# A rotary-embedding kernel on one core: the last load and the first store cut into four DMAs each, and one table copy moved to ScalarE

## The chip, the core and the metric

One core of a Trainium2 chip. The metric is device time in microseconds (us), the median over executions of one program; a profiled execution also gives its span, from the first to the last instruction, which is some 1.7 us shorter than the time. Most executions agree within 0.3%. Now and then one is 1.5 to 2.1 us slower: these are called slow runs and are left out wherever two kernels are compared.

## The reference

```python
x: (8, 8, 1024, 64) float32, freqs: (32,), positions: (1024,), scale = 0.5
angles = np.outer(positions * scale, freqs)             # (1024, 32)
cos, sin = np.cos(angles), np.sin(angles)
x_first, x_second = x[..., :32], x[..., 32:]
out = concatenate([x_first * cos - x_second * sin,
                   x_first * sin + x_second * cos], axis=-1)   # float32
```

16.8 MB are read and 16.8 MB written, and there is little arithmetic for each byte.

## The kernel before

The 64 heads are four units of 16. A unit is a tile of 128 partitions with 8192 elements in each (N = 8192), which is 32 KB of float32 a partition, 4.19 MB in all. The loads that GpSimd issues cast to fp16 on their way: units 1 to 3 and the first half of unit 0. Its second half comes as float32, issued by SyncE and ScalarE. VectorE multiplies and adds in fp16, ScalarE copies the result to a float32 tile OUT, and that is stored: units 0 and 1 from GpSimd, one DMA each, units 2 and 3 from SyncE in halves.

```python
    # ... tiles, and unit 0's second half to X0f by SyncE and ScalarE (cut)
    pin(nc.gpsimd.dma_start(out=Xf[0][:, :NH], in_=xv[0][:, :NH]))
    # ... small constants for the tables (cut)
    for u in range(1, NU):
        pin(nc.gpsimd.dma_start(out=Xf[u], in_=xv[u]))
    # ... angles, sine and cosine on few rows (cut)
    for g in range(0, G, 2):                 # 8 rounds: TensorE spreads the tables over the partitions
        ps = spread.tile([P, 2, 2, W], FP32, tag="g")
        # ... two matmuls (cut)
        if g in (0, 4):
            pin(nc.vector.tensor_copy(out=dst, in_=ps))
        else:
            pin(nc.scalar.copy(out=dst, in_=ps))
    pin(nc.scalar.copy(out=Xf[0][:, NH:], in_=X0f[:, :NH]))

    for u in range(NU):
        OUT = xout.tile([P, N], FP32, tag="O")       # 3 buffers
        for s in range(2):
            # ... four VectorE instructions on half s of X[u] (cut)
            pin(nc.scalar.copy(out=OUT[:, ns], in_=Xf[u][:, ns]))
            if u >= NU // 2:
                pin(nc.sync.dma_start(out=ov[u][:, ns], in_=OUT[:, ns]))
        if u < NU // 2:
            pin(nc.gpsimd.dma_start(out=ov[u], in_=OUT))
```

The whole kernel:

## Time and profile before

| | before |
|---|---|
| time, median | 84.51 us (84.47 to 84.59) |
| span of the profiled execution | 82.8 us |
| VectorE, ScalarE busy | 73%, 49% |
| DMA queues' packets, share of 16 engines' time | 66.4 + 27.2 + 3.2 = 96.8% |
| landings of units 1, 2, 3 and of unit 0's store | 22.62, 32.32, 42.98, 52.74 us |

How to read it: two engines look half free, but the DMA engines are never free. The lines that carry this are in the prediction below. The number to keep is the distance between two landings, called a *step* here: 4.19 MB take 9.70 us when the stream runs well, and the step from unit 2 to unit 3, the last load, was 10.66 us.

One warning on the windows: a packet counts where it starts, with the bytes it writes. A load that casts thus shows 216 GB/s when it reads 432, and one microsecond can show a DMA share above 1 when many long packets start in it.

### The profile page before, as it was taken

Reading aid. Unit: us, or ns where it says so; the run is one execution under the profiler, and the core shown is the slowest. Engines: PE = TensorE matmul, PEld = TensorE weight load, DVE = VectorE, ACT = ScalarE, POOL = GpSimd, SP = SyncE. Lnnn points to the kernel's source line nnn. Section 1 sums busy time; section 2 is a strip of 40 time slices with the busy share of each in tenths; the row PEclk is TensorE's granted clock in tenths of the full one; section 3 lists DMA queues with packets and bytes.
Section 4 is the critical chain, followed back from the end, with each engine's and each line's share of the span. In section 5 each row is a group of like instructions: output and inputs, shape, how many; then the busy total and the mean of one; then the engine's idle time right before and its main releaser. Section 6 shows DMA issues by size and latency. Waiting matters only on the chain.

```text
span 82.8 us, 179 instructions
## 1 busy us (share of the span) xinstructions
PE 7.0 (8%) x18; PEld 2.7 (3%) x18; DVE 60.3 (73%) x40; ACT 40.1 (49%) x18; POOL 4.6 (6%) x14
## 2 busy tenths in 40 slices
PE   0011799200000000000000000000000000000000
PEld 0011233000000000000000000000000000000000
DVE  0306276999999999999999999999999997000000
ACT  0602159999960690294088049209606912950000
POOL 4920000000000002000000200000000000000000
PEclk9999999975555555555555555555555555555555
DMA  2899998997999899699979989999899999999991
GB/s 40 335 326 269 293 333 182 253 238 150 246 253 198 182 253 238 143 253 253 127 301 459 507 348 412 507 443 420 380 436 420 412 420 436 444 420 436 428 428 55
DMA packets 1874, 26.22 MB, mean 317 GB/s; under 512 B 338, under 2 KB 338, under 8 KB 338
## 3 DMA queue, kind: packets, MB, share of 16 engines
q0 software_dynamic: 864, 15.73, 66.4%
q1 hardware_dynamic: 720, 9.44, 27.2%
q10 hardware_dynamic: 290, 1.06, 3.2%
HBM read 16.79 MB, written 16.78 MB: 406 GB/s over the span
## 4 chain that ended last, share of the span: by engine, by line
DVE 55%; ACT 14%; issue 6%; DMA 6%; PE 5%; DVEq 1%; ACTq 0%
DVE pr L152 19%; DVE X L153 19%; DVE X L157 9%; DVE X L154 6%; DMA freq_row<-in_freqs_dram 6%; ACT T L139 5%; ACT OUT L160 4%; PE ps L129 4%; ACT X L140 4%; DVEq L195 1%; PE cfreq L97 1%; ACT tab L122 1%; DVE r L113 1%; DVE y L104 1%; ACTq L69 0%
## 5 line engine op out<-in xcount | busy, mean ns | idle before, releaser
L160 ACT CAST OUT<-X 128x4096 f32<-128x4096 f16 x8 | 28.8, 3606 | 24.2 <-DVE X L157 24.2
L152 DVE TENSOR_TENSOR pr<-X,T 128x4096 f16<-128x4096 f16 x8 | 18.3, 2292 | 1.0 <-ACT T L139 0.7
L153 DVE TENSOR_TENSOR X<-X,T 128x4096 f16<-128x4096 f16 x8 | 18.3, 2292 | 0.3
L154 DVE TENSOR_TENSOR X<-X,pr 128x2048 f16<-128x2048 f16 x8 | 9.8, 1225 | 0.3
L157 DVE TENSOR_TENSOR X<-pr,X 128x2048 f16<-128x2048 f16 x8 | 9.7, 1219 | 0.0
L139 ACT CAST T<-ps 128x1024 f16<-128x1024 f32 x6 | 5.7, 1030 | 2.6 <-PE ps L129 2.6
L129 PE MATMUL ps<-tab,sel 128*128 128x512 f16 x16 | 6.4, 584 | 2.2 <-ACT tab L122 2.2
L137 DVE CAST T<-ps 128x1024 f16<-128x1024 f32 x2 | 2.5, 1225 | 2.2 <-PE ps L129 2.2
L140 ACT CAST X<-X0f 128x4096 f16<-128x4096 f32 x1 | 3.7, 3651 | 0.0
L164 POOL DMA_DIRECT2D out_dram<-OUT x2 | 1.1, 536 | 40.3 <-ACT OUT L160 40.3
L95 DVE COPY sel<-one 128x2048 f16<-128x2048 f16 x1 | 0.7, 693 | 2.8 <-POOL one L87 2.8
L117 ACT ACTIVATE tab<-r 128x256 f16<-128x256 f32 x1 | 0.4, 416 | 4.3 <-DVE r L113 4.3
L129 PEld LDWEIGHTS <-sel 128*128 128x128 f16 x16 | 2.2, 138 | 6.0 <-issue 5.8
L117 ACT ACT_TABLE_LOAD x1 | 1.3, 1283 | 2.1 <-issue 2.1
L92 POOL DMA_DIRECT2D X<-in_x_dram x3 | 2.0, 658 | 0.0
L100 DVE CAST posf<-pos_i 128x8 f32<-128x8 int32 x1 | 0.2, 172 | 2.3 <-DMA pos_i<-in_positions_dram 2.3
L97 PE MATMUL cfreq<-freq_row,coef 1*128 1x32 f32 x2 | 0.6, 392 | 5.9 <-DMA freq_row<-in_freqs_dram 5.9
L104 DVE TENSOR_TENSOR y<-posf,cfreq 128x256 f32<-128x256 f32 x1 | 0.4, 422 | 0.5 <-PE cfreq L97 0.5
L83 POOL DMA_DIRECT2D X<-in_x_dram x1 | 0.7, 667 | 0.8 <-POOLq L181 0.8
L97 PEld LDWEIGHTS cfreq<-freq_row,coef 1*128 1x128 f32 x2 | 0.5, 305 | 5.8 <-issue 5.8
L122 ACT ACTIVATE tab<-ra,quarter 128x256 f16<-128x256 f32 x1 | 0.5, 507 | 0.0
L113 DVE SCALAR_TENSOR_TENSOR r<-m,y 128x256 f32<-128x256 f32 x1 | 0.4, 424 | 0.0
(10 smaller groups left out, 1.9 us busy)
## 6 DMA issues: line engine op xcount, KB each, us to landing
out_dram<-OUT POOLq DMA_DIRECT2D x2, 4096.0 KB, 20.8
out_dram<-OUT SPq DMA_DIRECT2D x4, 2048.0 KB, 11.6
X<-in_x_dram POOLq DMA_DIRECT2D x3, 2048.0 KB, 28.7
X0f<-in_x_dram SPq DMA_DIRECT2D x1, 1024.0 KB, 4.8
X<-in_x_dram POOLq DMA_DIRECT2D x1, 1024.0 KB, 11.7
X0f<-in_x_dram ACTq DMA_DIRECT2D x1, 1024.0 KB, 12.2
pos_i<-in_positions_dram ACTq DMA_DIRECT2D x1, 8.0 KB, 5.0
freq_row<-in_freqs_dram ACTq DMA_DIRECT2D x1, 0.1 KB
```

The source lines that it names most:

```text
L92: pin(nc.gpsimd.dma_start(out=Xf[u], in_=xv[u]))
L97: nc.tensor.matmul(out=cfreq, lhsT=coef, rhs=freq_row, start=True, stop=True)
L117: pin(nc.scalar.activation(out=tab[:, 0], in_=r, func=AF.Sin, bias=0.0, scale=-_TWO_PI_DN))
L129: nc.tensor.matmul(out=ps[:, i].rearrange("p t w -> p (t w)"), lhsT=sel[:, g + i].rearrange("s h q -> s (h q)"), rhs=tab.rearrange("s t k ...
L137: pin(nc.vector.tensor_copy(out=dst, in_=ps))
L139: pin(nc.scalar.copy(out=dst, in_=ps))
L140: pin(nc.scalar.copy(out=Xf[0][:, NH:], in_=X0f[:, :NH]))
L152: pin(nc.vector.tensor_tensor(out=pr, in0=Xs, in1=sin_b, op=ALU.mult))
L153: pin(nc.vector.tensor_tensor(out=Xs, in0=Xs, in1=cos_b, op=ALU.mult))
L154: pin(nc.vector.tensor_tensor(out=Xs[:, :, 0, :], in0=Xs[:, :, 0, :], in1=pr[:, :, 1, :], op=ALU.subtract))
L157: pin(nc.vector.tensor_tensor(out=Xs[:, :, 1, :], in0=pr[:, :, 0, :], in1=Xs[:, :, 1, :], op=ALU.add))
L160: pin(nc.scalar.copy(out=OUT[:, ns], in_=Xf[u][:, ns]))
```

## The change

The kernel is bound by its DMA stream, and the stream loses about one microsecond where loads turn to stores. The intent, as far as the diff tells it, was to shrink what is in flight there: unit 3 is loaded and unit 0 is stored in four DMAs each, with rows of 8 KB instead of 32 KB (counted in float32). Beside it one of VectorE's two table copies goes to ScalarE.

```diff
     for u in range(1, NU):
-        pin(nc.gpsimd.dma_start(out=Xf[u], in_=xv[u]))
+        parts = 4 if u == NU - 1 else 1
+        for i in range(parts):
+            c = slice(i * N // parts, (i + 1) * N // parts)
+            pin(nc.gpsimd.dma_start(out=Xf[u][:, c], in_=xv[u][:, c]))
...
-        if g in (0, 4):
+        if g == 0:
             pin(nc.vector.tensor_copy(out=dst, in_=ps))
...
         if u < NU // 2:
-            pin(nc.gpsimd.dma_start(out=ov[u], in_=OUT))
+            parts = 4 if u == 0 else 1
+            for i in range(parts):
+                c = slice(i * N // parts, (i + 1) * N // parts)
+                pin(nc.gpsimd.dma_start(out=ov[u][:, c], in_=OUT[:, c]))
```

## The prediction

> **What bounds the kernel now.** I read the page first (busy shares, the 40 slices, the DMA queues), then the chain of work that ended last, then the landings of single DMAs, then windows of one to ten microseconds, and at the end the packet records. The page:
>
> ```profile
> DVE  0306276999999999999999999999999997000000
> DMA  2899998997999899699979989999899999999991
> q0 software_dynamic: 864, 15.73, 66.4%
> q1 hardware_dynamic: 720, 9.44, 27.2%
> q10 hardware_dynamic: 290, 1.06, 3.2%
> HBM read 16.79 MB, written 16.78 MB: 406 GB/s over the span
> ```
>
> The VectorE line stops at four fifths of the span while the DMA line never stops, and the shares of the three queues add up to 96.8% of the 16 DMA engines' time. The rest, 3.2% of 82.8 us or 2.6 us, is the start (the first packet begins at 1.75 us) and the end (the last one ends at 81.5 us). So the DMA engines carry packets without a gap. 33.57 MB in 79.75 us is 421 GB/s.
>
> The chain of work names VectorE for 55% of the span, but it ends with the last ScalarE copy, which starts at 69.84 us and takes 3.60 us, and 9 us of stores are still to come. The issues by window show who waits at the end (stores of unit 3, first and second half; the columns are KB and us to landing):
>
> ```profile
> out_dram<-OUT SPq DMA_DIRECT2D x1, 2048.0 KB, 10.5
> ...
> out_dram<-OUT SPq DMA_DIRECT2D x1, 2048.0 KB, 8.4
> ```
>
> The first was issued at 66.47 us and lands at 77.0, the second at 73.47 and lands at 81.9. A half takes 4.86 us of the engines, so the second was moved straight after the first and had waited for it. Issue to first packet took 1.0 us where the queue was empty (0.74 to 1.75 us at the start), so VectorE and ScalarE could end some 2.5 us later and change nothing. The bound is the DMA stream alone, and a gain counts only if that stream gets shorter.
>
> Is the stream at one rate? The windows (columns PE, PEld, DVE, ACT, POOL, clock, DMA share, GB/s; a packet counts where it starts, and a load that casts to fp16 counts at its written half):
>
> ```profile
> 22.70:32.40 9.70, 0.00 (x0) 0.00 (x0) 9.53 (x7) 4.92 (x2) 0.54 (x1) 0.50 1.01 216
> 32.40:42.10 9.70, 0.00 (x0) 0.00 (x0) 9.56 (x7) 4.05 (x2) 0.00 (x0) 0.50 1.00 196
> ...
> 43.00:52.70 9.70, 0.00 (x0) 0.00 (x0) 9.56 (x6) 5.87 (x2) 0.53 (x1) 0.50 1.00 432
> ```
>
> Unit 2's load moves 216 GB/s of fp16, which is 432 of source; unit 0's store moves 432. Unit 3's load, the last one, manages 196 although its engines are just as busy. Single landings say the same: unit 1 at 22.62 us, unit 2 at 32.32, unit 3 at 42.98, unit 0's store at 52.74. The steps are 9.70, 10.66 and 9.76 us. So there is one blemish of 0.96 us, and it lies exactly where the loads end and the stores begin:
>
> ```profile
> 40.00:41.00 1.00, 0.00 (x0) 0.00 (x0) 1.00 (x2) 0.00 (x0) 0.00 (x0) 0.50 2.01 262
> 41.00:42.00 1.00, 0.00 (x0) 0.00 (x0) 0.97 (x2) 0.34 (x1) 0.00 (x0) 0.50 0.00 0
> 42.00:43.00 1.00, 0.00 (x0) 0.00 (x0) 1.00 (x1) 1.00 (x1) 0.00 (x0) 0.50 1.25 524
> ```
>
> All 16 engines start the last row of the load between 40.2 and 40.7 us and none starts another packet before 42.04. The packet records have the last row of each engine at 2.01 us on average and the one before at 1.41, where every other row took 1.227: 0.78 + 0.18 = 0.96 us, the step again. I see no other loss in the stream.
>
> **What the Trainium skill says.** "DMA: Bandwidth & Descriptors", section "Where 436 GB/s comes from", gives 435.2 GB/s as what the fabric lets 16 DMA engines move. The 432 GB/s above agree: in the steady parts nothing is left, so only the changeover can be gained. The same page, "Anatomy of one DMA", gives each DMA about 2.0 us of fixed cost, mostly the wait for the receipt. Six more DMAs would then be 12 us if exposed; but on one queue the trace shows landings 9.70 us apart for 4.19 MB, which is 432 GB/s with the completion inside, so it is hidden. "Why small descriptors are slow", also there, speaks of about 3 cycles a packet and 32 bytes a descriptor; against 8 KB that is little, and the trace agrees: 16 KB rows of one store follow each other every 0.607 us on an engine, 32 KB rows every 1.209. "SBUF — State Buffer", in its box on DVE blocking DMA, warns that GpSimd can't write descriptors while VectorE holds the shared port. Not seen here: both GpSimd stores were issued in 0.53 to 0.54 us while VectorE was 96% busy.
>
> **The change part by part.**
>
> *Six more DMAs on GpSimd.* Each costs GpSimd about 0.54 us. The three more loads end near 6.3 us instead of 4.7; the engines reach unit 3 at 32.3 us. The stores: the listing of the changed kernel's order has the second to fourth quarter wait for semaphores that units 0 to 2's loads used before. These land at 13, 22.6 and 32.3 us, so the last quarter is issued by about 33.9 us at the latest, and the engines reach it after 42. Worth 0.
>
> *More packets.* Unit 3's load and unit 0's store go from 128 rows each to 512, and there are 6 x 16 = 96 more semaphore packets: 768 + 96 = 864 more, so q0 should show 1,728. Rows: 16 KB against 32 KB costs 2 x 0.607 - 1.209 = 0.005 us a 32 KB row. With two and three times that for 8 KB, 0.010 to 0.015 us, over 8 rows an engine and two units: 0.16 to 0.24 us. Semaphores: an engine's next row comes 0.022 us later where one DMA ends on the load queue, 0.006 to 0.009 in the stores: 3 x 0.022 + 3 x 0.008 = 0.09 us. Sum: +0.25 to +0.33 us, all on the path, as the engines have no gap.
>
> *The changeover.* A store that SyncE issued at 52.33 us got its first packet at 55.82, when GpSimd's store had 32 KB rows in flight; 1.0 us is its issue, so an engine seems to have one to two rows committed ahead. My reading: near the end of the load an engine already fetches the store's first row from SBUF beside the load's last row from HBM, so the last load row gets only part of the read side, and the write side starves; 0.96 us is 0.79 of a 32 KB row's 1.209 us. If what is committed ahead is counted in rows, 8 KB rows lose a quarter: 0.24 us, a gain of 0.72. If it is counted in bytes, the gain is 0. I hold the first for likelier, some 60 to 40. This is the step on which the sign depends.
>
> *The table copy.* VectorE's copies take 1.23 us each, at 9.75 and 11.46; ScalarE's 1.03:
>
> ```profile
> L139 ACT CAST T<-ps 128x1024 f16<-128x1024 f32 x6 | 5.7, 1030 | 2.6 <-PE ps L129 2.6
> L137 DVE CAST T<-ps 128x1024 f16<-128x1024 f32 x2 | 2.5, 1225 | 2.2 <-PE ps L129 2.2
> ```
>
> ScalarE's first ends at 11.6 and it then waits until 12.31, so the moved copy fills that hole. With ScalarE's own spacing of 0.93 to 0.94 us (three in 2.80 us) the copy now at 12.31 starts near 12.48: the first product on VectorE, ScalarE's copy of X0f and everything after them come 0.17 us later. VectorE gets 1.23 us freer in a stretch where it waits for that copy anyway. Against 2.5 us of slack at the end: 0.
>
> *Sum.* Counted in rows: -0.72 + 0.29 = -0.4 us. Counted in bytes: +0.3 us.
>
> **The rivals.**
> (a) The changeover loss stays, as it is one of bytes in flight or of HBM turning from reads to writes: 84.8 us. For it speaks that all engines slow down together around 40 us; against it, that the slowdown begins before any store packet.
> (b) Rows of 8 KB at a pitch of 32 KB in memory run slower: unit 3 and unit 0 at 10% less would be +2 us, 86.5. Against it: X0f was loaded in just such rows and took 0.313 us each on a busy engine, a 64-byte packet of the other queue between two of them included, which is no loss.
> (c) VectorE or a buffer takes over as the bound: unit 3's output goes into unit 0's buffer, but unit 0's store lands at 52.7 and the buffer is wanted at 62.8. VectorE needs unit 3 at 55.7 and it lands near 42.6. Slack of 10 us or more, so I give this little.
> (d) The loss disappears wholly and rows cost nothing: 83.5 us.
>
> **Range and chances.** 84.51 - 0.4 in the likelier case, + 0.3 in the other: I say 84.2 us. The range is 83.6 (nearly all of the 0.96 us back) to 85.0 (nothing back and rows half as dear again as estimated). A verdict of faster needs 82.8, so 1.7 us, more than the one blemish holds; slower needs 86.2, which only (b) or something unseen gives. Chances: faster 0.03, same 0.93, slower 0.04.
>
> **What would show it.** The step from unit 2's landing to unit 3's last landing falls from 10.66 to about 10.0 us if rows count, and stays near 10.7 or more if bytes do; no whole microsecond near 41 us without a packet start; q0 with 1,728 packets; the stores of unit 0 within 9.76 + 0.2 us of the last load; the first product on VectorE near 13.5 us; the last store issued near 73.6 us, still behind another. I'd be wrong if small rows run below 432 GB/s, if the quarters wait on GpSimd, or if the end comes to hang on VectorE.

## The result, and the profile after

The time went from 84.51 us to 84.69 us (84.58 to 84.96), six fast runs each. The ratio is 1.0022, with a 95% interval of 1.0006 to 1.0037: the change costs about 0.2 us, within 2%. Ratios here and below are the mean time of one kernel's fast runs over that of the other's fast runs of the same rounds, so they are not quite the ratio of the medians quoted.

The page of the changed kernel; the lines are those that the prediction shows of before (queues: packets, MB, share of 16 engines):

```profile
DVE  0306416999999999999999999999999995000000
DMA  2899997997999798999999999989999899999991
...
q0 software_dynamic: 1728, 15.73, 67.1%
q1 hardware_dynamic: 720, 9.44, 27.1%
q10 hardware_dynamic: 290, 1.06, 3.2%
```

The 1,728 packets are there, and the same 15.73 MB took 67.1% of a span of 82.9 us where they had taken 66.4% of 82.8. The shares add up to 97.4%: still no gap. The same microseconds as before (columns PE, PEld, DVE, ACT, POOL, clock, DMA share, GB/s):

```profile
40.00:41.00 1.00, 0.00 (x0) 0.00 (x0) 1.00 (x2) 0.00 (x0) 0.00 (x0) 0.50 1.05 127
41.00:42.00 1.00, 0.00 (x0) 0.00 (x0) 0.97 (x2) 0.51 (x1) 0.00 (x0) 0.50 1.03 131
42.00:43.00 1.00, 0.00 (x0) 0.00 (x0) 1.00 (x1) 1.00 (x1) 0.00 (x0) 0.50 0.99 352
```

Before, the slow row was one packet, so that its slowness showed only as a hole. With short rows the same stretch is resolved four times as finely, and it is not a hole but a slope: for two microseconds the load ran at 127 to 131 GB/s of fp16, instead of the 217 that it showed from 36 to 38 us, with every engine busy. The loss was made visible, not made smaller. The landings of unit 3's four quarters, issued at 4.13, 4.65, 5.17 and 5.69 us (columns KB, us to landing):

```profile
X<-in_x_dram POOLq DMA_DIRECT2D x1, 512.0 KB, 30.6
X<-in_x_dram POOLq DMA_DIRECT2D x1, 512.0 KB, 32.6
X<-in_x_dram POOLq DMA_DIRECT2D x1, 512.0 KB, 34.6
X<-in_x_dram POOLq DMA_DIRECT2D x1, 512.0 KB, 37.4
```

That is 34.77, 37.23, 39.73 and 43.06 us in the trace's record of semaphores. The quarters follow each other by 2.46, 2.46 and 2.50 us, and the last one by 3.33. The step from unit 2 to the end of unit 3 is 10.75 us (before: 10.66), the step of unit 0's store 9.87 (before: 9.76). The two differences, 0.09 and 0.11 us, add up to the 0.2 us of the result; they come from one profile each, and the run of the table copy below shows that the second repeats well and the first does not.

### The profile page after: what moved, and what is told of

The parts are those of the page before. It is cut to its first block, busy times and chain, and to the rows that moved or that the text cites. A ratio compares the mean times of both kernels' runs of the same rounds, so it can differ in the third digit from the quotient of the medians.

```text
span 82.9 us, 192 instructions
## 1 busy us (share of the span) xinstructions
PE 6.9 (8%) x18; PEld 2.7 (3%) x18; DVE 59.1 (71%) x39; ACT 41.0 (49%) x19; POOL 7.8 (9%) x20
## 3 DMA queue, kind: packets, MB, share of 16 engines
q0 software_dynamic: 1728, 15.73, 67.1%
q10 hardware_dynamic: 290, 1.06, 3.2%
## 4 chain that ended last, share of the span: by engine, by line
DVE 54%; ACT 17%; issue 7%; DMA 5%; PE 3%; DVEq 1%; ACTq 0%
DVE X L156 19%; DVE pr L155 19%; DVE X L160 9%; ACT T L142 7%; DMA freq_row<-in_freqs_dram 5%; DVE X L157 5%; ACT OUT L163 4%; ACT X L143 4%; PE ps L132 2%; DVEq L201 1%; PE cfreq L100 1%; ACT tab L125 1%; DVE r L116 1%; DVE y L107 1%; ACTq L69 0%
## 5 line engine op out<-in xcount | busy, mean ns | idle before, releaser
L142 ACT CAST T<-ps 128x1024 f16<-128x1024 f32 x7 | 6.5, 1043 | 2.0 <-PE ps L132 2.0
L170 POOL DMA_DIRECT2D out_dram<-OUT x5 | 2.7, 537 | 37.0 <-ACT OUT L163 36.3
L95 POOL DMA_DIRECT2D X<-in_x_dram x6 | 3.5, 612 | 0.0
L140 DVE CAST T<-ps 128x1024 f16<-128x1024 f32 x1 | 1.2, 1225 | 1.7 <-PE ps L132 1.7
L83 POOL DMA_DIRECT2D X<-in_x_dram x1 | 0.7, 669 | 0.8 <-POOLq L187 0.8
```

The lines of the kernel that those rows point to most:

```text
L95: pin(nc.gpsimd.dma_start(out=Xf[u][:, c], in_=xv[u][:, c]))
L170: pin(nc.gpsimd.dma_start(out=ov[u][:, c], in_=OUT[:, c]))
```

## The experiments

Eleven kernels ran, one of them twice. All gave correct results. The times of before that stand beside each run are those taken on the same chip. Three theories were to be told apart:

- **P, read-ahead.** The engines read a part of the coming store beside the last rows of the load. The load slows down for as long as that takes. It happens when a store stands behind the load, and once.
- **R, rows.** As P, but what is read ahead is counted in rows, so short rows shrink it. This was the likelier case of the prediction.
- **T, turning.** Memory or engine pays each time that the direction turns from reads to writes. **E**, a cousin: the last rows of any queue of loads are slow by themselves. **W**, which comes in with the later runs: any store that waits behind a load slows its last rows, however small it is.

### One part of the change at a time

Only the loads:

```diff
+        parts = 4 if u == NU - 1 else 1      # loop as in the change; store and table copy as before
```

> Only unit 3's load is split into four DMAs of 8 KB rows. If the loss where loads end and stores begin counts bytes (theory P: the engines read a fixed amount of the coming store beside the last of the load), it stays: step from unit 2's landing to unit 3's last landing 10.7 to 10.8 us, and the kernel 0.05 to 0.15 us slower than before (24 rows more an engine at 0.003 us and 3 semaphores at 0.022 us are 0.14 us). If it counts rows of the load (theory R): step near 10.1 us and 0.4 us or more faster.

Measured: 84.59 us against 84.55, ratio 1.0004 (0.9987 to 1.002). Step to unit 3: 10.59 us, of which 0.14 are the shorter rows and the semaphores; so the loss is 10.59 - 9.69 - 0.14 = 0.76 us (9.69 is the step without any loss, measured below). R's 10.1 us and 0.4 us gained did not come.

Only the store:

```diff
+            parts = 4 if u == 0 else 1       # loop as in the change; loads and table copy as before
```

> Only unit 0's store is split into four DMAs of 8 KB rows. Theory P: the step to unit 3's landing stays 10.66 us, the store's own step grows from 9.76 to about 9.87 us, the kernel is about 0.1 us slower. Theory R, counting rows of the store: step near 10.0 us and 0.5 us faster. If e1 and e2 together make up the 0.2 us of the whole change, nothing is left for the table copy.

Measured: 84.77 us against 84.55, ratio 1.0027 (1.0014 to 1.0041). Of the three parts this is the only one whose interval leaves out no change at all. That of the loads alone reaches 1.002, so some of the cost can lie there too.

Only the table copy:

```diff
-        if g in (0, 4):
+        if g == 0:
```

> Only the table copy goes to ScalarE. Every theory: the last store is issued with some 2.5 us to spare, so the time is that of before within 0.05 us; the first product on VectorE starts 0.1 to 0.2 us later than before, counted from the start of the sine. More than 0.1 us of change would say that the end does hang on VectorE.

Measured: 84.61 us against 84.55, ratio 1.0008 (0.9996 to 1.0021), no difference that the runs can tell. VectorE's first product started 5.74 us after the sine (13.54 and 7.80 us) where it had been 5.61 (13.36 and 7.75), so 0.13 us later, and nothing came of it. VectorE and ScalarE have time to spare at the end, as the prediction read from the landings. This run also tells how well a step repeats, as its loads and stores are those of before. The store's step is the same, 9.75 us. The step to unit 3 is 10.60 us where the profile of before has 10.66; by the middle one of the 16 engines instead of the last it is 10.50 where before has 10.69. A difference of 0.1 to 0.2 us between two single profiles of this step therefore tells nothing.

### Four turns instead of one

The eight DMAs of the change, in another order on GpSimd: load quarter, store quarter, four times; q4(i) stands for the i-th quarter of the columns.

```diff
+    pin(nc.gpsimd.dma_start(out=Xf[3][:, q4(0)], in_=xv[3][:, q4(0)]))        # after units 1 and 2
...
+            for i in range(4):                                                # after unit 0's products
+                pin(nc.gpsimd.dma_start(out=ov[0][:, q4(i)], in_=OUT[:, q4(i)]))
+                if i < 3:
+                    pin(nc.gpsimd.dma_start(out=Xf[3][:, q4(i + 1)], in_=xv[3][:, q4(i + 1)]))
```

> The same eight DMAs as in the changed kernel, but in the order load quarter, store quarter, four times, so that loads turn to stores four times instead of once. Theory P: what is read ahead is read ahead once and stays ahead, so the loss comes once and the time is that of the changed kernel, 84.5 to 84.9 us. Rival T (memory or engine pays 0.9 us at each turn from reads to writes): three more turns, 84.7 + 2.7 = 87.4 us.

Measured: 84.85 us against 84.55, ratio 1.0034 (1.0022 to 1.0046). T wanted 87.4 us; it falls. Windows of this kernel, within the four quarters of unit 3's load (last column GB/s, fp16):

```profile
32.00:35.00 3.00, 0.00 (x0) 0.00 (x0) 2.93 (x4) 0.56 (x1) 0.97 (x2) 0.50 1.03 141
...
38.00:39.00 1.00, 0.00 (x0) 0.00 (x0) 1.00 (x1) 0.05 (x1) 0.00 (x0) 0.50 1.06 213
...
43.00:44.00 1.00, 0.00 (x0) 0.00 (x0) 0.97 (x2) 1.00 (x1) 0.00 (x0) 0.50 1.03 209
...
48.00:49.00 1.00, 0.00 (x0) 0.00 (x0) 0.97 (x2) 0.47 (x1) 0.00 (x0) 0.50 1.13 229
```

Only the first quarter is slow, though a store follows each of the four. Its step is 3.51 us; the other three loads, each counted from the landing of the store before it, take 2.37, 2.23 and 2.44. So the microsecond is paid once, at the first store, and it moved from 40 us to 33 us with that store: it does not belong to a time of the kernel.

The other way to more turns was to store unit 0 from SyncE, on a queue of its own, so that its rows alternate with those of unit 3:

```diff
+        if u == 0:
+            pin(nc.sync.dma_start(out=ov[u], in_=OUT))
```

> Unit 0's store is issued by SyncE on its own queue, so its rows alternate with those of unit 3's load, packet by packet, from about 33 us on. Theory P: the loss of about 0.9 us comes once, when the store begins, and the time is that of before within 0.3 us. Rival T (each turn from reads to writes costs): eight turns an engine instead of one, several us more.

Measured: 84.79 us against 84.51, ratio 1.003 (1.0014 to 1.0046). From 36 to 50 us packets of loads and stores alternate on the engines, and it costs 0.3 us, not several. T falls here too. The packet records have the loss where P expects it: the two load rows before the store's first row took 1.43 and 1.81 us on average, and every later one, each with a store row before it, 1.23.

### No store behind the load

GpSimd reads one element a partition of unit 3 before it issues the store, so the store can't be in the queue when the load ends.

```diff
+        if u == 0:
+            seen = tmp.tile([P, 1], FP16)
+            pin(nc.gpsimd.tensor_copy(out=seen, in_=Xf[3][:, :1]))
         if u < NU // 2:
             pin(nc.gpsimd.dma_start(out=ov[u], in_=OUT))
```

> The kernel before, but GpSimd reads one element a partition of unit 3 before it issues unit 0's store, so no store stands behind the last load. Theory P (the slow end of the load is the read-ahead of the store): the step from unit 2's to unit 3's landing falls from 10.66 to 9.70 us, and no row of the load takes over 1.3 us; the stream then stands still for 1 to 3 us until the store's first packet, so the time is 0.5 to 2.5 us longer than before. Rival E (the last rows of a load are slow by themselves): the step stays at 10.6 us or more.

Measured: 87.32 us against 84.51, ratio 1.0324 (1.0308 to 1.0339). The two loads of units 2 and 3, issued at 3.60 and 4.11 us (KB, us to landing), then the windows after them:

```profile
X<-in_x_dram POOLq DMA_DIRECT2D x1, 2048.0 KB, 28.9
X<-in_x_dram POOLq DMA_DIRECT2D x1, 2048.0 KB, 38.1
```

```profile
42.00:44.90 2.90, 0.00 (x0) 0.00 (x0) 2.87 (x2) 2.90 (x1) 2.18 (x2) 0.50 0.00 0
45.00:54.70 9.70, 0.00 (x0) 0.00 (x0) 9.56 (x7) 3.81 (x2) 0.53 (x1) 0.50 0.98 416
```

Landings at 32.49 and 42.18 us: the step is 9.69 us and all 128 rows of unit 3 took 1.226 or 1.227 us. Without a store behind it the end of the load is not slow, so E falls: the 0.96 us are the store's doing. But the loss is the cheaper evil. The engines stood still from 41.85 us (end of the load's last packet) to 44.98 (start of the store's first), and the kernel lost 2.8 us, a little more than the 2.5 us that was allowed for. Of the 3.13 us of pause, 1.70 are the gate itself, GpSimd's copy; a quicker gate was not tried. The stores after the pause were also a little slower: the eight rows of unit 0 took each engine 1.23 us apiece on average instead of 1.21, 0.15 us in all. The 416 GB/s of the window overstate this, as five of its packets had started just before 45.00.

### Shorter rows in the store

```diff
+            o4 = ov[0].rearrange("p (a b c) -> p b a c", a=4, b=4)     # a=16: 512 bytes
+            s4 = OUT.rearrange("p (a b c) -> p b a c", a=4, b=4)
+            for i in range(4):
+                pin(nc.gpsimd.dma_start(out=o4[:, i], in_=s4[:, i]))
```

> Unit 0's store in four DMAs with rows of 2 KB, the load as before. Theory P with a read-ahead limited in bytes, some 25 KB an engine: the step to unit 3's landing stays 10.5 to 10.7 us; the store's own step grows by 15 rows more for each 32 KB at about 0.003 us, 8 times, plus semaphores, 0.4 us. If the read-ahead is limited in descriptors and the limit is under 12, the step falls below 10.5 us.

> Unit 0's store in four DMAs with rows of 512 bytes. If the read-ahead is limited in bytes, the step to unit 3's landing stays 10.5 to 10.7 us; if in descriptors and the limit is under 48, it falls towards 9.7 us. The store itself gets slower: 63 rows more for each 32 KB at 0.003 us, 8 times, is 1.5 us, so 86 us or more, or much more if such rows cost more than that.

Measured with 2 KB: 84.83 us against 84.51, ratio 1.0041 (1.0024 to 1.0058), step to unit 3 10.58 us, the store's step 10.14 (before: 9.76). With 512 bytes: 88.94 us, ratio 1.0522 (1.0506 to 1.0538), step to unit 3 10.46 us, the store's step 14.63. The loss stays at 0.77 us or more (10.46 less the 9.69 of the run without a store) while the rows shrink 64-fold. Shorter rows are no way to be rid of it, and they have a price of their own: in the middle of its store the last kernel moved only 276 GB/s.

```profile
48.00:54.00 6.00, 0.00 (x0) 0.00 (x0) 5.90 (x4) 3.61 (x1) 0.00 (x0) 0.50 1.00 276
```

The trace has these pieces as packets of 4 KB, so it does not show in what units they are read.

### How much of the store counts

If the loss is the reading of store data, a small store behind the load should cost little. The first columns of unit 0's store are issued early, the rest waits for unit 3 as in the run above.

```diff
+            pin(nc.gpsimd.dma_start(out=ov[0][:, :cols], in_=OUT[:, :cols]))   # cols = 256, 512, 1024
+            # ... tile seen, as above (cut)
+            pin(nc.gpsimd.tensor_copy(out=seen, in_=Xf[3][:, :1]))
+            pin(nc.gpsimd.dma_start(out=ov[0][:, cols:], in_=OUT[:, cols:]))
```

> As the gate run, but 1 KB a partition of unit 0's store (8 KB for each DMA engine) is issued early and so stands behind the last load; the rest waits for unit 3. Theory P (what is lost is the time in which the engines read the store ahead, 27 KB a us for an engine): the step from unit 2's to unit 3's landing is 9.69 + 0.30 = 10.0 us. Rival W (any store behind a load makes its last rows slow): the step is 10.5 to 10.7 us.

> The same with 2 KB a partition, 16 KB for each DMA engine, behind the last load. Theory P: 9.69 + 0.60 = 10.3 us. Rival W: 10.5 to 10.7 us.

> The same with 4 KB a partition, 32 KB for each DMA engine, behind the last load. Theory P with a read-ahead of about 25 KB an engine: the loss is full, 10.55 to 10.7 us, as in the kernel before, where 256 KB an engine stood behind it. If the read-ahead had no limit of its own it would be 9.69 + 1.2 = 10.9 us. Rival W: 10.5 to 10.7 us.

Their times (86.77, 86.50 and 89.21 us) contain the pause and say nothing; the steps are what counts. Units 2 and 3 with 8 KB for each DMA engine behind the load, then with 16 KB (issues near 3.60 and 4.12 us; KB, us to landing):

```profile
X<-in_x_dram POOLq DMA_DIRECT2D x1, 2048.0 KB, 28.5
X<-in_x_dram POOLq DMA_DIRECT2D x1, 2048.0 KB, 37.7
```

```profile
X<-in_x_dram POOLq DMA_DIRECT2D x1, 2048.0 KB, 28.7
X<-in_x_dram POOLq DMA_DIRECT2D x1, 2048.0 KB, 38.5
```

By the trace's landings the steps are 9.68 and 10.36 us. 16 KB cost 0.67 us, close to the 0.60 expected, and an unlimited amount, the kernel before, costs 0.97 (10.66 - 9.69): with one profile each, this fits P, in which the loss grows with what stands behind the load and then levels off. The packet records point the same way: with 16 KB behind it, the load's last row but one took 1.83 us on average and the last row 1.23, as fast as any, where the kernel before has 1.41 and 2.01. The slow stretch was over before the load was. W falls, as 8 KB disturb nothing. But 8 KB cost nothing, where P wanted 0.30 us. That is a miss: the simple rule, bytes of store over the engine's rate, does not hold for the first 8 KB, and I have no tested reason. A threshold between 8 and 16 KB is not excluded.

The run with 32 KB is inconclusive. Its profile is disturbed from the start (unit 0's first half lands at 14.00 us instead of 12.95, through one late engine out of 16, and unit 3 at 44.79). Taking the middle of the 16 engines' landings instead of the last, its step is 10.56 us, where the kernel before has 10.69 by the same count; that fits a levelling off near 25 KB, but one disturbed run doesn't show it.

### The store alone, again

> A second look at the kernel with only unit 0's store split, as its first profile fell in the slow state. Theory P: step to unit 3's landing 10.5 to 10.7 us as before, the store's own step 9.85 to 9.90 us instead of 9.76, rows of 8 KB following each other on an engine every 0.304 to 0.307 us.

Measured (one look): 84.77 us beside 84.67 of before. The store's step is 9.87 us, as expected and as in the whole change. The step to unit 3 is 10.96 us (landings 32.15 and 43.11), outside what was expected. So with long rows in the load and 8 KB rows in the store the loss is 1.27 us in this profile, against 0.97 and 0.91 in the two with 32 KB rows on both sides (before, and the table copy). With 8 KB on both sides it is 10.75 - 9.69 = 1.06 us, of which 0.14 are the load's own shorter rows and semaphores. Over all the row sizes tried the loss lies between some 0.8 and 1.3 us, in one profile each. Whether it depends on the row size within these bounds is not shown. By the middle engine, untouched loads and stores have a step of 10.69 and 10.50 us, this kernel 10.93 and, in its disturbed first profile, 10.71; and its fast runs were 0.12 to 0.35 us slower than before, where the two steps of this profile would make it 0.41. What can be said is that it is nowhere near a quarter of a microsecond, as R wanted.

No experiment beat the kernel before: the best, the loads alone, equals it. The DMA engines move what they can, and the one loss left in the stream cost more to avoid than to bear, in the ways tried here.

## Why the prediction was right or wrong

The time fell into the range, but the single figure pointed the wrong way: 0.3 us faster was written and 0.2 us slower came. That the range held is no merit of the likelier case: the range was drawn around both.

- **What bounds the kernel: right.** The queues fill 97.4% of the engines' time after, 96.8% before. The table copy alone, 0.13 us later on VectorE, changed nothing. The last store was issued at 73.31 us and landed 4.85 us after the one before it, so it had waited for that one as before.
- **Six more DMAs on GpSimd: right.** The four stores were issued at 24.14, 24.67, 31.35 and 32.60 us. The last waited 0.71 us for unit 2's landing, as the order of semaphores had it. The engines reached them at 42. Nothing came of the 12 us, an estimate, that they would cost if exposed.
- **More packets, +0.25 to +0.33 us: right.** 8 KB rows of the load follow each other on an engine every 0.3045 us, which is 1.218 us for four instead of 1.208 for a row of 32 KB; times 8 rows that is 0.08 us, and three semaphores of 0.022 us make it 0.14. The store took 0.11 us more. Together 0.25.
- **The changeover: the step that failed, and with it the sign.** "If what is committed ahead is counted in rows, 8 KB rows lose a quarter: 0.24 us, a gain of 0.72", held likelier "some 60 to 40". The term was -0.72 us; it measured -0.05: 0.97 us before, and 10.75 - 9.69 - 0.14 = 0.92 after, no more apart than two profiles of the same transfers (0.97 and 0.91). The prediction's own test said so: a step of 10.0 us if rows count, of 10.7 or more if bytes do, and 10.75 came. The kernel with short rows in the load alone (0.76) and the one with short rows in the store alone (1.27) lose it as well, and down to 512 bytes no row size brings it near a quarter. -0.05 + 0.25 is +0.2 us, and 84.69 - 84.51 is 0.18.
- **The reading behind it: supported, not complete.** That the slow end of the load comes from the store behind it is shown (no store, no loss; a store of 16 KB an engine, less loss), and that it comes once and not at each turn is shown too. That the engines read the store ahead of the load's last rows is the explanation that predicted these; nothing in the trace shows the read side by itself. One thing it doesn't explain: 8 KB behind the load cost nothing. And that what is read ahead is a fixed number of bytes, some 25 KB an engine, is not shown: the runs exclude that it shrinks in step with the rows, and no more.
- **Rival (a), the loss stays, 84.8 us:** this is what happened, within 0.1 us. Of its two reasons, turning from reads to writes was refuted by the run with four turns; bytes in flight stays. **Rivals (b), (c), (d):** none came. 8 KB rows of the load ran at 430 GB/s (4.19 MB in 32 x 0.3045 = 9.74 us), no buffer or engine became the bound, and the loss did not vanish.

## What to carry to other kernels

When the DMA queues fill the span at one rate, look at the distance between landings of equal transfers. A step that stands out is what is left to gain, and before anything is built on it, one run that takes away its supposed cause tells whether the cause is the right one. Here one run with the store held back would have shown that the store causes the slow end, and one with short rows in the store alone that rows are not what it counts. Cutting a transfer that already ran at full rate into smaller rows cost some 0.03 us here for each DMA of 1 MB, and bought nothing, as nothing waited for the pieces.

## What the Trainium skill lacked or had wrong

- "DMA: Bandwidth & Descriptors": no section of it tells that the last rows of a load slow down when the first store stands behind them: 10.66 us instead of 9.69 for 4.19 MB, once in the kernel, and not again at three more turns from loads to stores. No page has it.
- The same page, "Specifications", names 512 bytes as the least transfer for line rate. A store in pieces of 512 bytes, 2 KB apart, moved 276 GB/s in its middle; 4.19 MB took 14.63 us, against 10.14 with pieces of 2 KB, 9.87 with rows of 8 KB and 9.76 with rows of 32 KB.
- The same page's "Anatomy of one DMA" puts the fixed cost of a DMA near 2 us. In the run that held the store back, where it was exposed, it came to less: 0.33 us from the load's last packet to its landing (41.85 to 42.18) and 1.10 us from the store's issue to its first packet (43.88 to 44.98), 1.43 us together. On a queue that stays full, one more DMA cost 0.02 to 0.04 us, shorter rows included.
